# First batch of a rotary score kernel: eight-head groups with two row slots per step, and the third batch of k requested earlier

## The chip, the cores and the metric

The kernel runs on one core of one Trainium2 chip. The metric is device time in microseconds (µs): the median of several runs of the whole kernel. A profile of one execution is at hand; its span runs from the first to the last instruction, and its times count from the start of that span. All sizes are given in binary units (1 MB is 1024 KB), as the profile gives the sizes of transfers.

## What is computed

q and k have the shape 16 batches x 512 positions x 16 heads x 64 values, in float32. Both are rotated (rotary embedding), and then every position's q is multiplied with every position's k, head by head:

```
q1, q2 = q[..., :32], q[..., 32:]
q_rot = concatenate([q1*cos - q2*sin, q1*sin + q2*cos])      # k_rot likewise
scores = einsum('bshd,bthd->bsht', q_rot, k_rot)             # 16 x 512 x 16 x 512, float32
```

The output is 256 MB and the inputs are 64 MB, so the kernel moves much and computes little for each byte.

## The kernel before, in words

The 512 positions of a batch are split over 128 partitions of 4 positions each: partition p holds positions 4p to 4p+3. C is 4, the number of these row slots c. There are 64 steps `i`; from batch 1 on, step i is batch i // 4 and slot i % 4.

**One step from batch 1 on.** The rope of one slot of q (or k) is three VectorE (DVE) instructions (lines 149, 150, 154), which rotate the slot in place. TensorE (PE) transposes it in two groups `g` of four 128x128 blocks, each into a PSUM tile `bank` (line 170; two such buffers). A copy (line 185) takes each bank to `qT` or `kT` in SBUF, on ScalarE (ACT) or on DVE. `scores(i, p, st)` handles two heads: PE multiplies (line 201) into the PSUM tile `ps` (three buffers), and ACT copies ps to the staging tile `st` (line 208). After eight scores a 4 MB store goes out (line 188).

**The staging tiles.** `stage` has three buffers of 4 MB. The first two are `st_first`. The third first serves as `early`, which holds q and k of batch 0 until they are used; after that it too is a staging buffer. The third step waits until the stores of the first have landed.

**Batch 0** is treated differently, so that the first store can leave before all of batch 0 has arrived. A unit n (0 to 3) is a group of G = 4 heads in all four row slots, and it is loaded, roped and transposed as a unit: first unit 0 of k and of q (0.5 MB each), then units 1 to 3 (1.5 MB each), line 67. Step i of batch 0 computes all the scores of unit i: score p is row slot p // 2 and head pair p % 2 of the unit. After every second score a store of 1 MB leaves (line 211): 128 partitions, each with one run of 4 heads x 512 values x 4 bytes = 8 KB. So batch 0 has 16 stores.

**Order.** Nothing is reordered by a planner: instructions stand on each engine in the order in which the code is written (`manual_schedule`), and each engine works through its own in that order. In batch 0 the order is set by the loop over i and p: a list `dve` of rope halves, pieces of which are run at fixed p, and a list `nxt` of the two units to be transposed with ACT copies at p = 2 and p = 6. Beside unit i + 1 of k and q, step i also ropes slot i of batch 1's k, called ("k", C+i) in the code; it is transposed at p = 0 and 1 of the following step, with copies by DVE.

**Queues.** All loads and stores that matter here are issued by SyncE (SP), in the order of the code, and an issue that has to wait holds up those behind it. The order on SP in the first batch is: the four loads of batch 0, k of batch 1, q of batch 1 (all without a wait), two 1 MB stores, k of batch 2, four 1 MB stores, q of batch 2, ten 1 MB stores, k of batch 3, and then the 4 MB stores with two 2 MB loads in every batch. From batch 6 on a few loads go in parts through GpSimd's queue (`load_around`); the change does not touch them.

Of the kernel before, what the change touches and what calls it, by code (L numbers as in the profile page):

```python
# [10 lines left out]
def kernel(  # L11
# [8 lines left out]
    nc = tc.nc  # L20
# [7 lines left out]
    C = S // P  # L28
    HP = H // 2
    NST = B * C  # L30
    G = H // C
# [15 lines left out]
    o_v = out.rearrange("b (p c) h t -> b c p h t", c=C)  # L47
# [65 lines left out]
    def load(which, b):  # L113

        if b >= B:
            return
        t = in_pool.tile([P, C, H * D], fp32, tag=which + "_in", name=which + "_sb")
        batches[which, b] = t
        if (which, b) in RELIEVED:
            load_around(which, b, t)  # L120
        else:
            nc.sync.dma_start(t.rearrange("p c (h d) -> p c h d", h=H), dram[which][b])

    def rope(which, n):


        part = part_pool.tile([P, H * D], fp32, tag="part", name="part")
        if n < C:
            x = units[which, n]
            sv, k1, k2 = "p c (g j) -> p c g j", {"j": HD}, {"j": D}  # L130
            cs = cos_t.unsqueeze(2).to_broadcast((P, C, 2 * G, HD))
            ss = ss_v.unsqueeze(2).to_broadcast((P, C, G, D))
            pv = part.rearrange("p (c g j) -> p c g j", c=C, j=D)
            x5 = x.rearrange("p c (h x j) -> p c h x j", x=2, j=HD)
            p5 = part.rearrange("p (c h x j) -> p c h x j", c=C, x=2, j=HD)
            adds = [(x5[:, :, :, y], p5[:, :, :, 1 - y]) for y in range(2)]
        else:
            x = batches[which, n // C][:, n % C]
            sv, k1, k2 = "p (g j) -> p g j", {"j": HD}, {"j": D}
            cs = cos_t[:, n % C].unsqueeze(1).to_broadcast((P, 2 * H, HD))  # L140
            ss = ss_v[:, n % C].unsqueeze(1).to_broadcast((P, H, D))
            pv = part.rearrange(sv, **k2)
            x4 = x.rearrange("p (h x j) -> p h x j", x=2, j=HD)
            swapped = bass.AP(part.tensor, part.offset + HD, [part.ap[0], (D, H), (-HD, 2), (1, HD)])
            adds = [(x4, swapped)]
        xs, xc = x.rearrange(sv, **k2), x.rearrange(sv, **k1)

        def products():
            nc.vector.tensor_tensor(pv, xs, ss, op=mult)  # L149
            nc.vector.tensor_tensor(xc, xc, cs, op=mult)  # L150

        def sums():
            for y, z in adds:
                nc.vector.tensor_tensor(y, y, z, op=add)  # L154

        return [products, sums]

    kT = {}
    qT = {}

    def transposed(which, n, g, copy):


        bank = ps_t_pool.tile([P, 4, P], fp32, tag="ps_t", name="bank")
        for x in range(4):
            if n < C:
                src = units[which, n][:, x, P * g : P * (g + 1)]
            else:
                src = batches[which, n // C][:, n % C, P * (4 * g + x) : P * (4 * g + x + 1)]
            nc.tensor.transpose(bank[:, x, :], src, ident)  # L170
        src = bank
        if which == "q":
            if n not in qT:
                qT[n] = qt_pool.tile([P, HP, P], fp32, tag="qT", name="qT_t")
            dst = qT[n][:, 4 * g : 4 * g + 4, :]
        else:
            b = n // C
            if b not in kT:
                kT[b] = kt_pool.tile([P, HP, S], fp32, tag="kT", name="kT_t")
            if n < C:  # L180
                dst = kT[b][:, 2 * n + g].rearrange("p (t c) -> p t c", c=C)
                src = bank.rearrange("p c t -> p t c")
            else:
                dst = kT[b][:, 4 * g : 4 * g + 4, P * (n % C) : P * (n % C + 1)]
        copy(out=dst, in_=src)  # L185

    def store(i, st):
        nc.sync.dma_start(o_v[i // C, i % C], st)

    def scores(i, p, st):  # L190

        ps = ps_s_pool.tile([P, 2, S], fp32, tag="ps_s", name="ps")
        b = i // C
        if b == 0:
            c, hp = divmod(p, 2)
            lhs, rhs = qT[i][:, C * hp + c], kT[0][:, 2 * i + hp]
        else:
            lhs, rhs = qT[i][:, p], kT[b][:, p]
        for r in range(2):
            po, rh = ps[:, r, :], rhs[64 * r : 64 * r + 64, :]  # L200
            nc.tensor.matmul(  # L201
                out=po, lhsT=lhs[64 * r : 64 * r + 64, :], rhs=rh, start=True, stop=True
            )
        so, si = st[:, 2 * p : 2 * p + 2, :], ps
        if b > 0:
            so = so.rearrange("s r (t c) -> s r t c", c=C)
            si = si.rearrange("s r (c t) -> s r t c", c=C)
        nc.scalar.copy(out=so, in_=si)  # L208
        if b == 0 and p % 2 == 1:
            c = p // 2  # L210
            nc.sync.dma_start(o_v[0, c, :, G * i : G * (i + 1)], st[:, G * c : G * (c + 1)])
        elif b > 0 and p == HP - 1:
            store(i, st)

    def tr_act(which, n):
        for g in range(2):
            transposed(which, n, g, nc.scalar.copy)

    def run(ops):
        for op in ops:  # L220
            op()

    with tc.manual_schedule():
        for t, src in ((cos_t, cos), (sin_t, sin)):
            nc.scalar.dma_start(t, src.rearrange("(p c) j -> p c j", c=C))
        for head, heads in ((0, G), (G, H - G)):
            load_units("k", head, heads)
            load_units("q", head, heads)
        load("k", 1)
        load("q", 1)  # L230
        make_identity(nc, ident)
        nc.scalar.copy(out=ss_t[:, :, 0, :], in_=sin_t)
        nc.scalar.mul(ss_t[:, :, 1, :], sin_t, -1.0)
        for which in ("k", "q"):
            run(rope(which, 0))
            tr_act(which, 0)


        for i in range(C):
            st = st_first[i] if i < 2 else stage_pool.tile([P, H, S], fp32, tag="stage", name="st")  # L240
            if i < C - 1:
                dve = rope("k", i + 1) + rope("q", i + 1) + rope("k", C + i)
                nxt = [("k", i + 1), ("q", i + 1)]
            else:
                dve = rope("q", C) + rope("k", C + i) + rope("q", C + 1) + rope("k", 2 * C)
                nxt = [("q", C), ("k", C + i)]
            for p in range(HP):
                scores(i, p, st)
                if p in (0, 1) and i > 0:
                    run(dve[:1])  # L250
                    dve = dve[1:]
                    transposed("k", C + i - 1, p, nc.vector.tensor_copy)
                if p == 3 and i < 2:
                    load("kq"[i], 2)
                if p in (2, 6):
                    m = len(dve) - (4 if p == 2 else 2) - (2 if i == C - 1 else 0)
                    run(dve[:m])
                    dve = dve[m:]
                    tr_act(*nxt.pop(0))
            run(dve)  # L260
        load("k", 3)


        for i in range(C, NST):
            tr = {}
            if i + 1 < NST:
                tr[1], tr[3] = ("q", i + 1, 0), ("q", i + 1, 1)
            if i + C < NST:
                tr[5], tr[6] = ("k", i + C, 0), ("k", i + C, 1)
            dve = []  # L270
            if i + 2 < NST:
                dve += rope("q", i + 2)
            if i + 1 + C < NST:
                dve += rope("k", i + 1 + C)
            st = stage_pool.tile([P, H, S], fp32, tag="stage", name="st")
            for p in range(HP):
                scores(i, p, st)
                if p not in tr:
                    continue
                if tr[p][0] == "q":  # L280
                    run(dve[:1])
                    dve = dve[1:]
                    transposed(*tr[p], nc.vector.tensor_copy)
                else:
                    transposed(*tr[p], nc.scalar.copy)
            run(dve)
            if i % C == C - 2:
                load("q", i // C + 2)
            elif i % C == C - 1:
                load("k", i // C + 3)  # L290
# [30 lines left out]
```

## Time and profile before

| what | value |
|---|---|
| median of 3 runs | 793.13 µs (792.9 to 793.66) |
| span of the profiled execution | 790.4 µs |
| median less span, taken as what lies around the span | 2.7 µs |
| PE busy | 684.4 µs (87%) |
| DVE busy | 544.7 µs (69%) |
| ACT busy | 562.0 µs (71%) |
| moved by DMA | 336.18 MB (decimal), mean 425 GB/s |
| HBM read, written | 67.24 MB, 268.44 MB (decimal) |

The profile gives no second time for the profiled execution itself: what it shows is the span, and 790.4 + 2.7 µs is taken as its own time. The page cuts the span into 40 equal slices of 19.8 µs. Beside the engines' rows it has a row with the busy share of the 16 DMA engines in tenths (9 is 90% or more) and a row of what they moved. The timeline lists instructions in order of time; its rows for SP are the issues of transfers, and a row that merges several ("x10") has the time from the first issue to the end of the last. The trace also holds one record for each DMA packet, with its start, duration and size. One partition's run of a load or store is one packet, so the 1 MB stores have packets of 8 KB, the 2 MB loads of a whole batch 16 KB, and the 4 MB stores 32 KB. At the end of each transfer every one of the 16 engines has a small record of 4 bytes, the signal that its share is done.

### The profile page before, as it was taken

How to read it: one execution, taken by the hardware profiler on the slowest of the kernel's cores; microseconds unless marked ns; L12 is line 12 of the kernel's file. 1: busy time of each engine (PE TensorE's matmuls, PEld its weight loads, DVE VectorE, ACT ScalarE, POOL GpSimd, SP SyncE). 2: the span in 40 equal slices, each digit the busy share in tenths (PEclk: the TensorE clock that was granted, in tenths of full speed). 3: DMA queues.
4: the chain of work that ended last, by engine and by line, in shares of the span. 5: the costliest groups of instructions: out<-in, count | busy, mean ns of one | idle time of the engine just before them, and what ended most of it. 6: DMA issues, size and time to landing. Idle time of an engine off the chain costs nothing.

```text
span 790.4 us, 7750 instructions
## 1 busy us (share of the span) xinstructions
PE 684.4 (87%) x3072; PEld 296.4 (38%) x3072; DVE 544.7 (69%) x516; ACT 562.0 (71%) x647; POOL 11.9 (2%) x24
## 2 busy tenths in 40 slices
PE   4989998988988889798996989889899798799960
PEld 2444443433433334343342433334334343344420
DVE  6999988666766678576785767667678487587400
ACT  3888886865857768486785866777577586588770
POOL 0000000000001000000000001000000000000000
PEclk9999999998999999898998989999899899899995
DMA  9999999999999999999999999999999999999997
GB/s 357 417 425 439 429 430 435 425 435 436 429 429 428 413 432 419 433 423 438 433 427 436 426 432 429 422 432 424 430 432 427 436 429 432 430 432 434 432 429 340
DMA packets 18836, 336.18 MB, mean 425 GB/s; under 512 B 2312, under 2 KB 3592, under 8 KB 4616
## 3 DMA queue, kind: packets, MB, share of 16 engines
q1 hardware_dynamic: 16704, 325.46, 96.4%
q0 software_dynamic: 1808, 10.10, 3.1%
q8 instruction: 24, 0.39, 0.2%
q10 hardware_dynamic: 288, 0.13, 0.1%
q14 instruction: 12, 0.10, 0.0%
HBM read 67.24 MB, written 268.44 MB: 425 GB/s over the span
## 4 chain that ended last, share of the span: by engine, by line
DMA 49%; PE 40%; ACT 5%; DVE 3%; issue 1%; ACTq 0%; SPq 0%; DVEq 0%
DMA out_dram<-st 46%; PE ps L201 30%; PE bank L170 10%; ACT st L208 5%; DMA q_sb<-in_q_dram 2%; DVE part L149 1%; DMA early<-in_k_dram 1%; DVE q_sb L150 0%; DVE k_sb L154 0%; DVE k_sb L150 0%; DVE q_sb L154 0%; DVE early L150 0%; DVE kT_t L185 0%; ACTq L316 0%; DVE early L154 0%
## 5 line engine op out<-in xcount | busy, mean ns | idle before, releaser
L208 ACT COPY st<-ps 128x1024 f32<-128x1024 f32 x512 | 495.7, 1020 | 192.6 <-DMA out_dram<-st 109.8
L201 PE MATMUL ps<-kT_t,qT_t 64*128 64x512 f32 x2048 | 544.0, 649 | 67.0 <-ACT st L208 67.0
L201 PEld LDWEIGHTS ps<-kT_t,qT_t 64*128 64x128 f32 x2048 | 183.6, 196 | 256.2 <-issue 133.3
L185 DVE COPY qT_t<-bank 128x512 f32<-128x512 f32 x118 | 81.6, 691 | 193.9 <-PE bank L170 193.9
L170 PEld LDWEIGHTS bank<-ident,q_sb 128*128 128x128 f32 x480 | 54.2, 149 | 99.0 <-issue 96.4
L170 PEld LDWEIGHTS bank<-ident,k_sb 128*128 128x128 f32 x480 | 50.3, 140 | 96.4 <-DVE k_sb L150 39.5
L170 PE MATMUL bank<-ident,q_sb 128*128 128x128 f32 x480 | 85.1, 304 | 0.9 <-PE ps L201 0.9
L170 PE MATMUL bank<-ident,k_sb 128*128 128x128 f32 x480 | 78.5, 286 | 1.6 <-DVE qT_t L185 1.2
L185 ACT COPY kT_t<-bank 128x512 f32<-128x512 f32 x122 | 72.4, 598 | 6.4 <-PE bank L170 6.4
L154 DVE TENSOR_TENSOR k_sb<-k_sb,part 128x1024 f32<-128x1024 f32 x60 | 73.5, 1225 | 2.1
L150 DVE TENSOR_TENSOR q_sb<-q_sb,cos_t 128x1024 f32<-128x1024 f32 x60 | 73.5, 1225 | 2.1
L150 DVE TENSOR_TENSOR k_sb<-k_sb,cos_t 128x1024 f32<-128x1024 f32 x60 | 73.5, 1225 | 2.0
L149 DVE TENSOR_TENSOR part<-q_sb,ss_t 128x1024 f32<-128x1024 f32 x60 | 73.5, 1225 | 2.0
L149 DVE TENSOR_TENSOR part<-k_sb,ss_t 128x1024 f32<-128x1024 f32 x60 | 73.0, 1216 | 0.9 <-DMA k_sb<-in_k_dram 0.7
L154 DVE TENSOR_TENSOR q_sb<-q_sb,part 128x1024 f32<-128x1024 f32 x60 | 72.9, 1216 | 0.0
L170 PE MATMUL bank<-ident,early 128*128 128x128 f32 x64 | 10.5, 315 | 12.4 <-DVE early L154 10.5
L170 PEld LDWEIGHTS bank<-ident,early 128*128 128x128 f32 x64 | 8.3, 161 | 17.4 <-issue 13.4
L149 DVE TENSOR_TENSOR part<-early,ss_t 128x1024 f32<-128x1024 f32 x8 | 9.8, 1222 | 5.8 <-DMA early<-in_k_dram 5.7
L98 POOL DMA_DIRECT2D q_sb<-in_q_dram x3 | 2.3, 752 | 620.2 <-PE bank L170 446.2
L154 DVE TENSOR_TENSOR early<-early,part 128x512 f32<-128x512 f32 x16 | 10.3, 687 | 0.2
L150 DVE TENSOR_TENSOR early<-early,cos_t 128x1024 f32<-128x1024 f32 x8 | 9.8, 1225 | 0.3
L185 ACT COPY qT_t<-bank 128x512 f32<-128x512 f32 x10 | 5.7, 629 | 3.2 <-PE bank L170 3.2
(12 smaller groups left out, 15.9 us busy)
## 6 DMA issues: line engine op xcount, KB each, us to landing
out_dram<-st SPq DMA_DIRECT2D x60, 4096.0 KB, 24.7
k_sb<-in_k_dram SPq DMA_DIRECT2D x13, 2048.0 KB, 28.3
q_sb<-in_q_dram SPq DMA_DIRECT2D x12, 2048.0 KB, 26.5
out_dram<-st SPq DMA_DIRECT2D x16, 1024.0 KB, 13.8
q_sb<-in_q_dram POOLq DMA_DIRECT2D x3, 1920.0 KB, 27.8
k_sb<-in_k_dram POOLq DMA_DIRECT2D x2, 1920.0 KB, 43.3
early<-in_k_dram SPq DMA_DIRECT2D x1, 1536.0 KB
early<-in_q_dram SPq DMA_DIRECT2D x1, 1536.0 KB
```

Of the source, the lines that this page charges most:

```text
L98: nc.gpsimd.dma_start(dst, src)
L149: nc.vector.tensor_tensor(pv, xs, ss, op=mult)
L150: nc.vector.tensor_tensor(xc, xc, cs, op=mult)
L154: nc.vector.tensor_tensor(y, y, z, op=add)
L170: nc.tensor.transpose(bank[:, x, :], src, ident)
L185: copy(out=dst, in_=src)
L201: nc.tensor.matmul(out=po, lhsT=lhs[64 * r : 64 * r + 64, :], rhs=rh, start=True, stop=True)
L208: nc.scalar.copy(out=so, in_=si)
```

## The change

Batch 0 no longer goes unit by unit. `order[i]` lists for each step two units and two row slots: step 0 takes units 0 and 1 (heads 0 to 7) in slots 0 and 1, step 1 the same units in slots 2 and 3, step 2 units 2 and 3 in slots 0 and 1, step 3 the same in slots 2 and 3. Within a step the four scores of the lower unit come first (p = 0 to 3: two slots of two head pairs), then those of the upper one. A store leaves when the upper unit has finished a slot, after p = 5 and after p = 7: 2 MB, with runs of 8 heads, 16 KB. Batch 0 so has 8 stores in place of 16. The number of scores, ropes, transposes and copies stays the same.

The order by hand is now the table `plan`: after score (i, p) the listed operations follow. Two units' ropes come together, the transposes of batch 1's k come at p = 0 and 1 of the following step as before, and k of batch 2 is requested directly after q of batch 1, ahead of the first store. q of batch 2 follows the two stores of step 0.

```diff
+    E8 = 2 * G
+    order = [
+        [(2 * (i // 2) + u, 2 * (i % 2) + c, hp) for u in range(2) for c in range(2) for hp in range(2)]
+        for i in range(C)
+    ]
     def scores(i, p, st):
...
         if b == 0:
-            c, hp = divmod(p, 2)
-            lhs, rhs = qT[i][:, C * hp + c], kT[0][:, 2 * i + hp]
+            u, c, hp = order[i][p]
+            lhs, rhs = qT[u][:, C * hp + c], kT[0][:, 2 * u + hp]
+            at = E8 * (c % 2) + G * (u % 2) + 2 * hp
...
-        so, si = st[:, 2 * p : 2 * p + 2, :], ps
+        so, si = st[:, at : at + 2, :], ps
...
-        if b == 0 and p % 2 == 1:
-            c = p // 2
-            nc.sync.dma_start(o_v[0, c, :, G * i : G * (i + 1)], st[:, G * c : G * (c + 1)])
+        if b == 0 and u % 2 == 1 and hp == 1:
+            g = i // 2
+            nc.sync.dma_start(
+                o_v[0, c, :, E8 * g : E8 * (g + 1)], st[:, E8 * (c % 2) : E8 * (c % 2 + 1)]
+            )
...
         load("k", 1)
         load("q", 1)
+        load("k", 2)
...
+        plan = {
+            (0, 3): [("rope", "k", 1), ("act", "k", 1), ("rope", "q", 1), ("act", "q", 1)],
+            (0, 7): [("load", "q", 2), ("rope", "k", C)],
+            (1, 0): [("dve", "k", C, 0)],
+            (1, 1): [("dve", "k", C, 1), ("rope", "k", 2), ("rope", "q", 2)],
+            (1, 5): [("act", "k", 2)],
+            (1, 6): [("act", "q", 2)],
+            (1, 7): [("rope", "k", C + 1)],
+            (2, 0): [("dve", "k", C + 1, 0)],
+            (2, 1): [("dve", "k", C + 1, 1), ("rope", "k", 3), ("rope", "q", 3)],
+            (2, 3): [("act", "k", 3), ("act", "q", 3)],
+            (2, 7): [("rope", "k", C + 2)],
+            (3, 0): [("dve", "k", C + 2, 0)],
+            (3, 1): [("dve", "k", C + 2, 1), ("rope", "q", C), ("rope", "k", C + 3)],
+            (3, 4): [("act", "q", C)],
+            (3, 6): [("act", "k", C + 3)],
+            (3, 7): [("rope", "q", C + 1), ("rope", "k", 2 * C)],
+        }
         for i in range(C):
...
-            if i < C - 1:
-                dve = rope("k", i + 1) + rope("q", i + 1) + rope("k", C + i)
-                nxt = [("k", i + 1), ("q", i + 1)]
-            else:
-                dve = rope("q", C) + rope("k", C + i) + rope("q", C + 1) + rope("k", 2 * C)
-                nxt = [("q", C), ("k", C + i)]
             for p in range(HP):
                 scores(i, p, st)
-                if p in (0, 1) and i > 0:
-                    run(dve[:1])
-                    dve = dve[1:]
-                    transposed("k", C + i - 1, p, nc.vector.tensor_copy)
-                if p == 3 and i < 2:
-                    load("kq"[i], 2)
-                if p in (2, 6):
-                    m = len(dve) - (4 if p == 2 else 2) - (2 if i == C - 1 else 0)
-                    run(dve[:m])
-                    dve = dve[m:]
-                    tr_act(*nxt.pop(0))
-            run(dve)
+                for what, which, n, *g in plan.get((i, p), ()):
+                    if what == "rope":
+                        run(rope(which, n))
+                    elif what == "load":
+                        load(which, n)
+                    elif what == "act":
+                        tr_act(which, n)
+                    else:
+                        transposed(which, n, g[0], nc.vector.tensor_copy)
```

In `plan`, "rope" runs the three or four DVE instructions of a unit or slot, "act" its transposes with copies by ACT, "dve" one group of transposes with a copy by DVE, and "load" a request on SP.

More of the change, by code (lines that the diff above doesn't have):

```diff
@@ L194, in scores @@
         if b == 0:
-            c, hp = divmod(p, 2)
-            lhs, rhs = qT[i][:, C * hp + c], kT[0][:, 2 * i + hp]
+            u, c, hp = order[i][p]
+            lhs, rhs = qT[u][:, C * hp + c], kT[0][:, 2 * u + hp]
+            at = E8 * (c % 2) + G * (u % 2) + 2 * hp
         else:
-            lhs, rhs = qT[i][:, p], kT[b][:, p]
+            lhs, rhs, at = qT[i][:, p], kT[b][:, p], 2 * p
         for r in range(2):
```

## The prediction

> **What bounds the kernel now.** I read the page's rows by slices first. The sixteen DMA engines are full from the second slice to the last but one.
>
> ```profile
> DMA  9999999999999999999999999999999999999997
> GB/s 357 417 425 439 429 430 435 425 435 436 429 429 428 413 432 419 433 423 438 433 427 436 426 432 429 422 432 424 430 432 427 436 429 432 430 432 434 432 429 340
> q1 hardware_dynamic: 16704, 325.46, 96.4%
> ```
>
> So the time is start-up, plus bytes at about 430 GB/s, plus a tail. Nothing is won on PE, ACT or DVE; but whatever lets the DMA queue run empty is added to the end in full, for no later stretch has room to make it good. Next the engines' busy time in the stretch of the change, four windows of 20 µs (columns: PE, PEld, DVE, ACT, POOL with counts, then clock, DMA share, GB/s):
>
> ```profile
> 0.00:20.00 20.00, 8.51 (x35) 5.48 (x36) 13.95 (x15) 6.66 (x10) 1.39 (x7) 1.00 0.91 354
> 20.00:40.00 20.00, 20.00 (x105) 9.48 (x103) 19.40 (x21) 16.65 (x22) 0.00 (x0) 1.00 1.00 419
> 40.00:60.00 20.00, 17.91 (x93) 8.59 (x92) 19.62 (x22) 16.85 (x21) 0.00 (x0) 1.00 1.01 425
> 60.00:80.00 20.00, 18.75 (x92) 8.24 (x92) 19.66 (x19) 16.28 (x20) 0.00 (x0) 1.00 1.04 441
> ```
>
> DVE is busy 97 to 98% there: the ropes set when batch 0's stores can leave. A pause of DVE delays everything after it. The SP timeline shows when transfers are requested (first column; a merged row gives its first issue):
>
> ```profile
> 19.52 3.28 SPq L211 DMA_DIRECT2D out_dram<-st  x2
> 22.85 0.66 SPq L122 DMA_DIRECT2D k_sb<-in_k_dram  x1
> 24.29 9.39 SPq L211 DMA_DIRECT2D out_dram<-st  x4
> 33.73 0.84 SPq L122 DMA_DIRECT2D q_sb<-in_q_dram  x1
> 35.18 27.44 SPq L211 DMA_DIRECT2D out_dram<-st  x10
> 62.72 0.57 SPq L122 DMA_DIRECT2D k_sb<-in_k_dram  x1
> 73.69 20.37 SPq L188 DMA_DIRECT2D out_dram<-st  x3
> ```
>
> Stores wait for ACT's copies, not for SP. And DVE's timeline gives the starts of the ropes of k1, k2, q2, k3, q3 (units), the rows to be moved:
>
> ```profile
> 13.37 1.23 DVE L149 TENSOR_TENSOR part<-early,ss_t 128x1024 f32<-128x1024 f32 x1
> ...
> 24.84 1.22 DVE L149 TENSOR_TENSOR part<-early,ss_t 128x1024 f32<-128x1024 f32 x1
> ...
> 29.92 1.22 DVE L149 TENSOR_TENSOR part<-early,ss_t 128x1024 f32<-128x1024 f32 x1
> ...
> 37.54 1.22 DVE L149 TENSOR_TENSOR part<-early,ss_t 128x1024 f32<-128x1024 f32 x1
> ...
> 42.34 1.22 DVE L149 TENSOR_TENSOR part<-early,ss_t 128x1024 f32<-128x1024 f32 x1
> ```
>
> **DMA's side of the change.** The packet records give the commonest times: 27 ns for 0.5 KB, 46 for 1 KB, 121 for 3 KB, 309 for 8 KB, 611 for 16 KB, 1213 for 32 KB. Sixteen engines share 128 partitions, so a 2 MB load takes 128 x 611 / 16 = 4.89 µs, a 1 MB store 2.47, a 2 MB store 4.89, a 4 MB store 9.70; cos and sin together 0.43, a 0.5 MB load of batch 0 1.47, a 1.5 MB load 3.87.
>
> The runs: 2048 packets x 309 ns / 16 = 39.55 µs become 1024 x 611 / 16 = 39.10. **Gain 0.45 µs**, and 8 completion records of 9 ns per engine fall away, 0.07. I take 0.5.
>
> The Trainium skill ("DMA: Bandwidth & Descriptors", Anatomy of one DMA) fits 2.0 µs plus bytes / 436 GB/s to one transfer issued by GpSimd; by that, eight transfers fewer would save 16 µs. This trace disagrees: stores that stand in the queue follow one another at 2.45 µs per 1 MB (428 GB/s), so the fixed part is hidden and the sum goes by the packets.
>
> When does the queue run dry? With an effective start at 2.6 µs (first packet at 2.18, then a ramp), cos, sin, batch 0 and k and q of batch 1 end at 2.6 + 0.43 + 2 x 1.47 + 2 x 3.87 + 2 x 4.89 = 23.5; the completion records of that last load lie between 23.47 and 24.48. Eight 1 MB stores and k and q of batch 2 more give 53.05; the records there lie from 52.8 (eleven engines by 53.3) to 55.1 (the slowest). The account holds. **After the change:** k of batch 2 now ends at 28.4, the two stores of step 0 at 38.2, q of batch 2 at 43.1, the two stores of step 1 at **52.9**. The next bytes must be requested before that, less the delay from request to first packet: 0.74 to 2.18 = 1.4 µs at the start of the kernel. Below, it can't be less than a store's issue, 0.33; above, with the ramp, I allow 2. I take 1.4, the only row; the ends would make the first gap below 4.9 or 6.6.
>
> **Compute's side.** Durations: a unit's rope 3.85 µs (starts 9.52 and 13.37), a slot's 3.78, a DVE copy between them 0.50, ACT's copy of ps 0.94, of a bank 0.56, one score on PE 0.86 plus 0.2 after a change from transposes, a bank of four transposes 0.59. I walked all instructions in order with these through both codes. For the code before, the walk puts k of batch 3 at 62.83 (trace 62.72), the first 4 MB store at 73.87 (73.69), the fourth at 103.99 (103.74), and no dry queue.
>
> *Step 0.* The ropes up to slot 0 of batch 1's k keep their times: q1 ends at 21.04, that slot at 24.85. Scores 0 to 3 leave ACT by 21.3; the copies of k1's and q1's banks end at 23.7, scores 4 and 5 at 26.3. First store: **26.4** (was 19.52), data at 27.8. The earlier request of k of batch 2 covers just this: dry at 28.4, 0.6 µs in hand; it costs nothing else, being queued behind all loads that batches 0 and 1 need, and its issue of 0.66 µs falls where SP would wait for ACT anyway. Without it the queue would stand from 23.5. The second store goes out at 28.3.
>
> *The new wait.* DVE's next instruction is now the copy of batch 1's transposed k. PE makes that bank only after scores 4 to 7 of step 0 and one of step 1: ready at 28.6. DVE stands from 24.85, **3.75 µs**, and 1.15 more for the second bank (one more score and transpose). Before, k2's rope stood at 24.84 and the copies lay inside. What is queued behind is everything: k2's rope begins at 30.7 (24.84), q2's at 34.6 (29.92) and ends at 38.4.
>
> *Steps 1 and 2.* Step 1's first store comes at 35.0, its second, after k2's and q2's transposes, at 41.7; both are in time. The same wait returns at the start of step 2 (0.9 + 1.15 µs): k3 begins at 45.3 (37.54), q3 at 49.1 (42.34), ending at 53.0. Step 2's first store needs unit 3: transposes, two bank copies, scores 4 and 5, 4.6 µs more. It is requested at **57.55**, its data come at 58.95, and the queue ran dry at 52.9: **6.0 µs lost**. In the profile before, 1 MB stores of step 2 were requested from about 42 on, since unit 2 alone sufficed. The copy of step 2 that waited for step 0's stores (2.61 µs until 40.59) has no wait now: they land at about 40 (38.2 and the 1.8 that landing took there), and that copy comes at 43.6.
>
> *Step 3 and after.* DVE waits again for its copies (3.0 + 1.15 µs). From step 2's first store to step 3's first, compute takes 11.4 µs (57.55 to 68.97), the two stores between 9.8: 1.6 lost. Then two stores and k of batch 3 (14.7 µs) against 15.8 until the first 4 MB store at 84.76 (was 73.69): 1.1 lost. Steps now run at 10.04 µs against 9.71 for a 4 MB store: 0.33 lost twice, until the q load fills the queue again. Before, there were about 4 µs in hand at 73.69 (stores and k of batch 3 end at 77.8); the change delays compute there by 11.
>
> Sum: 6.0 + 1.6 + 1.1 + 0.3 + 0.3 = 9.3 lost, 0.5 gained. One correction: two engines run 1.5 and 2.1 µs behind the rest at 53 µs and so stand less in the first gap. If one of these ends the kernel, the loss is up to 2 smaller; the last store's records spread from 783.6 to 789.0, and I can't tell which engine is last. I take 0.6 off: **+8.2 µs**. The profiled execution has 790.4 + 2.7 around it; that is the median, 793.1, so 801.3.
>
> **The rivals.**
> 1. *Only the large gap counts* (0.15). The four small gaps fall away, by a compute that is a little quicker than walked or by lagging engines that never stand: 6.0 - 2 - 0.5 = +3.5, 796.6. For it: the small ones total 3.3 µs, and errors of 0.1 to 0.2 µs per step are seen in the check. Against: they come from differences of durations (10.04 against 9.71), which the check confirms.
> 2. *Not slower: the queue never runs dry* (0.06). One mechanism: DVE does not wait at the starts of steps 1 and 2, so that step 2's first store is requested before 51.5 (52.9 - 1.4). It decides from 6 µs earlier than walked; the two waits are 6.95 together, so both must vanish. Then only the packets count: -0.5, 792.6; at best, if all packets of the stretch from 20 to 60 µs ran at 430 GB/s in place of 422, -0.8 more. Against: PE's order puts those banks behind the scores, and in the profile before PE and ACT had no time to spare there.
> 3. *The first store is late too* (0.07). Only 0.6 µs of cover stands at 28.4; should the new run of transposes and scores take 4 µs longer, a gap of about 3 opens there and the rest is pushed back: +11.5, 804.6.
>
> Forecast 0.72: 801.3. The range takes in rivals 1 and 3: 796.5 to 804.6. A difference under 0.2% (1.6 µs) can't be told from no change in measurements of this kernel; rival 2 splits into same 0.04 and faster 0.02, the rest, 0.94, is slower.
>
> **What the changed profile would show.** Right: the DMA row drops to 7 or 8 in the third slice (39.5 to 59.3) and the GB/s there falls to about 300 (6 of 19.8 µs at 430), the two after it to some 400; step 2's first store is issued at 57 to 58; DVE has idle time ahead of line 185 (kT) released by PE, some 11 µs in all; the first 4 MB store is issued near 85; the slices from the sixth on are unchanged; span near 798.6. Wrong: a third slice at 9 and stores of step 2 issued before 52; a dip near 28 speaks for rival 3; a single dip, with full slices from the fourth on, for rival 1. What would overthrow it altogether is a changed packet time in the later slices, which nothing here moves.

## The result, and the profile after

| | before | after |
|---|---|---|
| median of 5 runs each, side by side | 793.13 µs (792.78 to 793.84) | 806.32 µs (805.21 to 806.58) |
| ratio, 95% interval | | 1.0161 (1.0149 to 1.0173) |
| span of the profiled execution | 790.4 µs | 804.7 µs |
| its own time | not shown | 806.47 µs |

The changed kernel is 13.2 µs slower, 1.6%. The forecast was 801.3 (796.5 to 804.6): the direction is right, the size is not, and the range misses the time by 1.7 µs. The spans differ by 14.3 µs and the medians by 13.2. For the kernel after, 1.8 µs lie around the span (806.47 less 804.7); with 1.8 in place of the 2.7 that the prediction took, the profiled execution of before ran about 0.9 µs quicker than its median, and the one of after 0.15 µs slower, which together is that difference. The steps below are set against the 14.3.

First the page of the kernel after, its rows by slices and the queue that holds the loads and stores:

```profile
DMA  9969999999999999999999999999999999999997
GB/s 351 430 269 390 415 395 415 429 430 438 423 434 425 390 428 426 437 431 424 437 433 428 430 433 427 402 435 421 436 432 429 437 425 432 432 432 432 429 434 333
q1 hardware_dynamic: 15552, 325.46, 95.1%
```

A slice is 20.1 µs now. The third one, from 40.2 to 60.4, has a 6 where before had a 9, and 269 GB/s. It is the only digit that moved, but the figures below it show more: 390 in the fourth slice, 395 in the sixth, 390 in the fourteenth. Next the requests on SP in the timeline of the kernel after (start, duration, and how many):

```profile
26.41 0.35 SPq L218 DMA_DIRECT2D out_dram<-st  x1
28.25 0.34 SPq L218 DMA_DIRECT2D out_dram<-st  x1
34.97 0.33 SPq L218 DMA_DIRECT2D out_dram<-st  x1
41.73 0.33 SPq L218 DMA_DIRECT2D out_dram<-st  x1
59.75 0.33 SPq L218 DMA_DIRECT2D out_dram<-st  x1
61.62 9.96 SPq L218 DMA_DIRECT2D out_dram<-st  x2
75.52 0.91 SPq L122 DMA_DIRECT2D k_sb<-in_k_dram  x1
87.00 0.33 SPq L188 DMA_DIRECT2D out_dram<-st  x1
```

The four stores of steps 0 and 1 were predicted at 26.4, 28.3, 35.0 and 41.7, and they came there. Step 2's first was predicted at 57.55 and came at 59.75. The first 4 MB store is at 87.00, 13.3 µs later than before; the prediction had 84.76. The DVE timeline of the kernel after shows why (the bracket is the idle time ahead of an instruction, and what ended it):

```profile
28.47 0.69 DVE L185 COPY kT_t<-bank 128x512 f32<-128x512 f32 x1 [3.62 <-PE bank L170]
30.12 0.69 DVE L185 COPY kT_t<-bank 128x512 f32<-128x512 f32 x1 [0.95 <-PE bank L170]
30.73 1.22 DVE L149 TENSOR_TENSOR part<-early,ss_t 128x1024 f32<-128x1024 f32 x1
...
42.97 0.69 DVE L185 COPY kT_t<-bank 128x512 f32<-128x512 f32 x1 [0.81 <-PE bank L170]
44.61 0.69 DVE L185 COPY kT_t<-bank 128x512 f32<-128x512 f32 x1 [0.95 <-PE bank L170]
45.22 1.22 DVE L149 TENSOR_TENSOR part<-early,ss_t 128x1024 f32<-128x1024 f32 x1
...
61.97 0.69 DVE L185 COPY kT_t<-bank 128x512 f32<-128x512 f32 x1 [5.32 <-PE bank L170]
```

DVE stands for the transposed k of batch 1 at the start of each step, and the ropes of k2 and k3 start at 30.73 and 45.22, as predicted (30.7, 45.3). Up to 53 µs the walk was right to 0.2 µs. What it missed stands in the windows of 2 µs of the kernel after (columns as in the prediction: engines, clock, DMA share, GB/s):

```profile
50.00:52.00 2.00, 0.23 (x3) 0.00 (x0) 1.93 (x3) 0.91 (x2) 0.00 (x0) 0.98 0.96 410
52.00:54.00 2.00, 0.99 (x5) 1.02 (x6) 1.97 (x3) 0.00 (x0) 0.00 (x0) 0.50 0.44 188
54.00:56.00 2.00, 2.00 (x9) 1.16 (x9) 1.93 (x3) 1.17 (x2) 0.00 (x0) 0.50 0.06 25
56.00:58.00 2.00, 2.00 (x8) 0.91 (x6) 0.65 (x1) 0.99 (x1) 0.00 (x0) 0.50 0.00 0
58.00:60.00 2.00, 2.00 (x10) 0.82 (x8) 0.00 (x0) 1.30 (x3) 0.00 (x0) 0.82 0.00 0
60.00:62.00 2.00, 2.00 (x14) 0.84 (x12) 0.03 (x1) 2.00 (x3) 0.00 (x0) 1.00 0.93 393
```

PE waits for the rope of q3 and is nearly idle until 53.0; its granted clock is then 0.50 until 58 and 0.82 between 58 and 60. The transposes and scores that step 2's first store needs run in just that time, and the DMA queue stands: nothing is requested, and its engines idle. What the clock does to them is seen on PE's timeline, in the eight transposes of k3 and the eight of q3:

```profile
49.17 1.06 PE L170 MATMUL bank<-ident,early 128*128 128x128 f32 x8 [2.68 <-DVE early L154]
53.01 1.94 PE L170 MATMUL bank<-ident,early 128*128 128x128 f32 x8 [2.78 <-DVE early L154]
```

**Where the 14.3 µs of span are**, from the packet records, as means over the 16 engines:

| term | µs |
|---|---|
| the queue stands, 52.9 to 60.6 | 7.3 |
| it stands again at 70.3 to 72.1 | 1.6 |
| and at 87.3, 97.5 and 107.6 | 0.8 |
| smaller stands | 0.2 |
| packets that took longer than the commonest of their size: 10.3 against 5.9 before | +4.4 |
| the sum of the commonest durations (fewer, longer packets) | -0.5 |
| idle engines after 770 µs | +0.3 |
| packet records that overlap on an engine: 3.8 against 4.0 before | +0.2 |
| sum | 14.3 |

In the profile of e10 below, the same kernel once more, the stands sum to 9.9 as here, the longer packets to +3.8 and the idle tail to +1.2: these two terms differ by 0.6 to 0.9 µs between two executions of one kernel.

### The profile page after: what moved, and what is told of

It reads as the page before. It is cut to its first block, busy times and chain, and to the rows that moved or that the text cites. A ratio compares the mean times of both kernels' runs of the same rounds, so it can differ in the third digit from the quotient of the medians.

```text
span 804.7 us, 7732 instructions
## 1 busy us (share of the span) xinstructions
PE 686.3 (85%) x3072; PEld 298.4 (37%) x3072; DVE 545.2 (68%) x516; ACT 563.3 (70%) x647; POOL 12.0 (1%) x24
## 4 chain that ended last, share of the span: by engine, by line
DMA 46%; PE 40%; ACT 5%; DVE 5%; issue 1%; ACTq 0%; DVEq 0%
DMA out_dram<-st 46%; PE ps L208 30%; PE bank L170 10%; ACT st L215 5%; DVE part L149 2%; DVE early L150 1%; DVE early L154 1%; DMA early<-in_k_dram 1%; DVE k_sb L154 0%; DVE k_sb L150 0%; DVE q_sb L150 0%; DVE q_sb L154 0%; DVE kT_t L185 0%; ACT kT_t L185 0%; ACTq L335 0%
## 5 line engine op out<-in xcount | busy, mean ns | idle before, releaser
L170 PEld LDWEIGHTS bank<-ident,k_sb 128*128 128x128 f32 x480 | 50.3, 140 | 96.5 <-issue 40.2
L154 DVE TENSOR_TENSOR q_sb<-q_sb,part 128x1024 f32<-128x1024 f32 x60 | 72.9, 1216 | 0.1
L170 PE MATMUL bank<-ident,early 128*128 128x128 f32 x64 | 11.3, 333 | 20.3 <-DVE early L154 17.7
L185 DVE COPY kT_t<-bank 128x512 f32<-128x512 f32 x6 | 4.2, 692 | 12.6 <-PE bank L170 12.6
L154 DVE TENSOR_TENSOR early<-early,part 128x512 f32<-128x512 f32 x16 | 10.3, 688 | 0.3
```

## The experiments

The theory was the prediction's: DVE's copies of batch 1's k, put ahead of the next ropes, make it wait for banks that PE makes only behind a run of scores; compute falls behind by more than the queue has in hand, the queue runs dry, and that is never made good. The rivals: the early request of k of batch 2 does it; the pairing does it, since a 2 MB store needs two units; the 16 KB runs do it (rival C). After the result two more questions came up: what PE's halved clock costs, and where the 4.4 µs of longer packets come from. Medians are set against the kernel before on the same chip: 793.08, 793.38 and 793.76 in the three groups (e1 to e4, e5 to e8, e9 to e11).

**e1: the early request alone.** The kernel before, with k of batch 2 requested right after q of batch 1.

```diff
         load("q", 1)
+        load("k", 2)
...
-                if p == 3 and i < 2:
-                    load("kq"[i], 2)
+                if p == 3 and i == 1:
+                    load("q", 2)
```

> The kernel before, with one part of the change alone: k of batch 2 is requested directly after q of batch 1. Theory A (the loss comes from DVE standing ahead of the kT copies, which makes compute late): compute keeps its times, the queue never runs dry, 793.1 within 0.7. Rival (a load of 2 MB ahead of the first stores pushes the early stores back and makes the third step wait for staging): step 2 waits up to 4.9 longer for the stores of step 0, up to 798.

Measured: 793.23 (792.25 to 794.15), ratio 1.0002 (0.9993 to 1.001); the queue never stands. Moving the request into a full queue costs nothing. It isn't the cause.

**e2: the changed kernel without the early request.** k of batch 2 follows step 0's two stores.

```diff
-        load("k", 2)
...
-            (0, 7): [("load", "q", 2), ("rope", "k", C)],
+            (0, 7): [("load", "k", 2), ("load", "q", 2), ("rope", "k", C)],
```

> The changed kernel, with k of batch 2 requested after the two stores of step 0 instead of ahead of the first. Theory A: the queue stands for about 4 near 24 to 28, but the stand before step 2's first store shrinks from 7.3 to about 3.3, since the same bytes are moved by the same late requests; total 806.3 within 1.5. Rival (each stand adds up; the early request is worth its cover): 806.3 + 4 = 810.

Measured: 806.54 (806.48 to 806.62), 1.017 (1.0157 to 1.0183), the changed kernel's time. The page of e2:

```profile
DMA  9798999999999999999999999999999999999997
GB/s 356 324 370 377 406 408 415 427 438 431 423 437 425 393 430 427 436 434 423 440 430 430 432 429 429 416 430 422 433 430 432 432 425 435 430 434 429 430 437 325
```

The hole moves: 4.1 µs at 23.4 to 27.7 (the second slice), then only 2.1 at 58.6, 1.7 at 70.8 and three of 0.3. They sum to 8.8 µs, and the span is 804.7 in both kernels. A queue that stood early has more left to send later, so the later hole is smaller. The request is harmless, and under a compute that is late anyway it is worth nothing.

**e3: the ropes back in front of the copies.** The changed kernel, with DVE's list in an order that keeps it busy: the next unit's rope before the first copy, the first instruction of the other unit's rope between the two ("products"; "sums" are the rest).

```diff
-            (0, 7): [("load", "q", 2), ("rope", "k", C)],
-            (1, 0): [("dve", "k", C, 0)],
-            (1, 1): [("dve", "k", C, 1), ("rope", "k", 2), ("rope", "q", 2)],
+            (0, 7): [("load", "q", 2), ("rope", "k", C), ("rope", "k", 2)],
+            (1, 0): [("dve", "k", C, 0), ("products", "q", 2)],
+            (1, 1): [("dve", "k", C, 1), ("sums", "q", 2)],
...
```

Steps 2 and 3 are changed in the same way. Pairs, 2 MB stores and the early request stay.

> The changed kernel with DVE's order turned back: k2's rope (and k3's, and q of batch 1's first) goes ahead of the two kT copies, and the second copy stands between the two halves of the next rope. Pairs of units, 2 MB stores, 16 KB runs and the early request all stay. Theory A: DVE does not stand, step 2's first store is issued near 50.6 instead of 59.75, the first 4 MB store near 73.6 instead of 87.0, the queue never runs dry, 792.6 within 1. Rival B (stores that need two units are the cause): the queue still runs dry before step 2, 797 to 806. Rival C (packets of 16 KB and engines in step are slower): 795 to 798 without any stand.

Measured: 793.46 (792.0 to 795.84, 12 runs), 1.001 (1.0 to 1.0021). The page of e3:

```profile
DMA  9999999999999999999999999999999999999997
GB/s 355 430 426 434 428 433 431 424 438 434 428 430 430 419 434 415 436 423 433 438 422 437 433 427 434 412 434 418 435 426 428 440 428 427 429 438 432 429 437 310
```

And its requests on SP, step 2's first store, k of batch 3 and the first 4 MB stores:

```profile
50.35 0.33 SPq L218 DMA_DIRECT2D out_dram<-st  x1
63.34 1.13 SPq L122 DMA_DIRECT2D k_sb<-in_k_dram  x1
73.33 20.36 SPq L188 DMA_DIRECT2D out_dram<-st  x3
```

Step 2's first store leaves before the queue is dry (52.9), the 4 MB store is 13.7 µs earlier than in the changed kernel, and the queue never stands. The whole loss is gone with the order on one engine alone; it decides for the theory. (Four of the 12 runs lie at 795.1 to 795.8, the others at 792.0 to 793.9; the profile is of one of the latter, and what sets the four apart is open.) The 0.5 µs of longer runs are not to be seen in it: 793.46 against 793.08.

**e4: no pairing of stores.** The changed kernel, but 1 MB leaves whenever a unit's slot is ready, so batch 0 has 16 stores of 8 KB runs again.

```diff
-        if b == 0 and u % 2 == 1 and hp == 1:
+        if b == 0 and hp == 1:
...
-                o_v[0, c, :, E8 * g : E8 * (g + 1)], st[:, E8 * (c % 2) : E8 * (c % 2 + 1)]
+                o_v[0, c, :, G * u : G * (u + 1)], st[:, E8 * (c % 2) + G * (u % 2) : E8 * (c % 2) + G * (u % 2 + 1)]
```

> The changed kernel's order of work, but each unit's slot leaves as soon as it is copied, in 16 stores of 1 MB with 8 KB runs. Theory A: stores leave earlier, compute stays late; the stand before step 2's upper unit shrinks to about 3, but stands appear before the stores of step 3 and the first 4 MB store (near 83 to 88), and the total stays at 806 within 1.5. Rival B (pairing is the cause): most of the loss goes, 794 to 800.

Measured: 805.81 (805.48 to 806.44), 1.0162 (1.0149 to 1.0175); span 804.7. The stands are now 2.4 at 57.5, 1.5 at 70, 1.4 at 74, 3.6 at 84 to 87 and two of 0.3, 9.4 in all. Smaller stores start earlier and fill part of the first hole, and the time shows up as another hole ahead of the first 4 MB store. Neither the pairing nor the 16 KB runs are the cause.

**e5: 2 MB in two stores of 8 KB runs.** Issued together, after the upper unit.

```diff
-            nc.sync.dma_start(
-                o_v[0, c, :, E8 * g : E8 * (g + 1)], st[:, E8 * (c % 2) : E8 * (c % 2 + 1)]
-            )
+            for x in range(2):
+                nc.sync.dma_start(
+                    o_v[0, c, :, E8 * g + G * x : E8 * g + G * (x + 1)],
+                    st[:, E8 * (c % 2) + G * x : E8 * (c % 2) + G * (x + 1)],
+                )
```

> The changed kernel with each 2 MB store of batch 0 cut into two of 1 MB (8 KB runs) that are requested one after the other at the same moment. Theory A (late compute): nothing moves but 0.45 of packet time, 806.3 within 1. Rival C (16 KB runs or large stores are themselves slower): 804 or less.

Measured: 807.82 (805.5 to 808.62), 1.0178 (1.0161 to 1.0194). It isn't a clean test: the lower half waits only for its own copies, so the first store left at 20.61 instead of 26.41, and in the profiled execution the first rope began 0.4 µs later (6.12 against 5.72). It gives no sign for rival C, which needed 804 or less, but the effect of the packet size alone isn't isolated by it.

**e6 and e11: PE kept warm.** The changed kernel with 20 and 22 transposes of the identity into the bank, ahead of k3's and q3's own transposes (which then overwrite them). e11 is the same kernel once more, beside e10, the changed kernel once more, on one chip.

```diff
+    WARM = {("k", 3, 0): 20, ("q", 3, 0): 22}
...
+        for x in range(WARM.get((which, n, g), 0)):
+            nc.tensor.transpose(bank[:, x % 4, :], ident, ident)
```

> The changed kernel with 20 and 22 additional transposes of the identity (overwritten by the real ones) ahead of the transposes of k3 and q3, so that PE does not stand while DVE ropes them. If the halved granted clock of PE at 52 to 58 is what put step 2's first store 2.2 later than the 57.55 of the prediction, that store now goes out near 57.7, the stand before it shrinks from 7.3 to about 5.3, and all later requests come 2 earlier: 804.3 within 0.8. Rival (the clock does not matter; the prediction's walk was off elsewhere): 806.3.

> The changed kernel once more, beside the next one on the same chip: 806.3 within 1, stands of 9 to 10.5 in all, packet records longer than before's by 3.5 to 5.5 for each engine.

> The changed kernel with the additional transposes that keep PE busy, once more: if the halved clock is worth the 2.6 by which step 2's first store came earlier, 2 to 3 below the changed kernel of this call. Rival (it only moves stands about): the same as the changed kernel within 1.

Measured: e6 804.32 (802.98 to 806.23), 1.014 (1.0123 to 1.0157); e10 806.53 (806.02 to 807.25), 1.0166 (1.0151 to 1.0181); e11 803.74 (803.33 to 804.29), 1.013 (1.0115 to 1.0145). The windows of e11:

```profile
50.00:52.00 2.00, 2.00 (x19) 2.00 (x20) 1.97 (x3) 0.35 (x1) 0.00 (x0) 1.00 1.00 426
52.00:54.00 2.00, 1.76 (x15) 1.39 (x15) 1.93 (x3) 0.88 (x2) 0.00 (x0) 1.00 0.27 115
54.00:56.00 2.00, 2.00 (x10) 0.84 (x10) 1.97 (x2) 1.26 (x3) 0.00 (x0) 1.00 0.04 8
56.00:58.00 2.00, 2.00 (x12) 0.77 (x8) 0.15 (x1) 2.00 (x3) 0.00 (x0) 1.00 0.30 131
```

The clock stays at 1.00 and step 2's first store is requested at 56.89, 2.8 µs before e10's 59.72 and near the 57.55 of the prediction. The stands fall from 9.9 to 7.2 µs and the time by 2.8 (806.53 to 803.74, and the ranges don't overlap). Not all of that is the clock: in the profiled executions 0.47 µs of the earlier store was there before the first added transpose (the first copy of k starts at 27.98 in e11, at 28.45 in e10). From the start of q3's transposes to the request it is 4.46 µs in e11 and 6.74 in e10, so the halved clock costs 2.3 µs on this chain; 2.8 is what the medians show.

**e7: one stand, elsewhere.** The kernel before, with 44 small copies on ACT, whose result nobody reads, ahead of step 6, so that a single 4 MB store is late.

```diff
+            if i == C + 2:
+                for _ in range(44):
+                    nc.scalar.copy(out=scratch[:, 64:96], in_=cos_t[:, 0, :])
```

> The kernel before with 44 small additional ACT copies ahead of step 6's, some 9 in all, so that the queue runs dry once, before the store of step 6 (near 97 to 104), and with nothing else changed. It asks whether a stand costs more than its length. If a stand costs its length alone: median = 793.1 + the stand read from the trace (some 6). If the 16 DMA engines, restarted together, then work in step and stretch one another's packets where loads and stores meet: 2 to 4 more than the stand, with the packet records of 100 to 290 longer than in the kernel before.

Measured: 804.71 (804.1 to 805.31), 1.0141 (1.0124 to 1.0157), span 803.5. The windows of e7, 4 µs each, around the stand and behind it:

```profile
92.00:96.00 4.00, 0.00 (x0) 0.00 (x0) 0.00 (x0) 3.62 (x15) 0.00 (x0) 0.50 0.97 418
96.00:100.00 4.00, 3.98 (x10) 1.72 (x12) 0.82 (x2) 2.81 (x3) 0.00 (x0) 0.50 0.21 90
100.00:104.00 4.00, 4.00 (x20) 1.67 (x16) 3.90 (x4) 2.88 (x4) 0.00 (x0) 0.91 0.00 0
104.00:108.00 4.00, 4.00 (x21) 1.89 (x22) 2.53 (x3) 3.85 (x5) 0.00 (x0) 1.00 0.31 131
116.00:120.00 4.00, 4.00 (x24) 1.68 (x20) 2.66 (x3) 3.48 (x5) 0.00 (x0) 1.00 0.68 266
```

The queue stands for 9.7 µs (mean of the engines, 96.6 to 107.1) instead of the 6 that were aimed at: PE idled here too and restarted at 0.50. The last row is no second stand: a packet is counted in the window in which it starts, the 16 engines began their 32 KB packets just before 116 µs (115.57 to 115.72), and the packet records show next to no idle time from 112 to 124 (0.03 µs). The span grew by 13.2: 9.7 of stand, 2.5 of longer packets, 0.9 at the tail. Between medians it is 11.3, the firmer number, for the profiled execution was the longest of e7's four. So with nothing else changed a stand of 9.7 costs 1.7 to 3.5 µs more than its length, and packets lengthen in a kernel that has neither pairs nor 16 KB stores.

**e8: the kernel before with the changed DVE order.** The two lines that run one rope instruction before each copy are taken out.

```diff
                 if p in (0, 1) and i > 0:
-                    run(dve[:1])
-                    dve = dve[1:]
                     transposed("k", C + i - 1, p, nc.vector.tensor_copy)
```

> The kernel before with one part of the change alone: DVE makes the two kT copies of a step ahead of the next rope, instead of between its halves; DVE's order is then that of the changed kernel, while units, 1 MB stores and requests stay as before. Theory A: DVE stands for PE, the first 4 MB store goes out near 81.7 instead of 73.7, the queue stands for some 5.7 in all (near 66, 79, 92 and 102), and with 2 to 4 of stretched packets the total is 799 to 803. Rival B (pairing is the cause, DVE's order alone is harmless): 793 to 795.

Measured: 806.16 (804.39 to 807.99), 1.0162 (1.0142 to 1.0182), above the 799 to 803 that was expected. The waits of the changed kernel and of e8 up to 110 µs have these rows (total, times, longest):

```profile
DVE kT_t L185 <- PE bank L170: 12.6, 6, 5.3
DVE kT_t L185 <- PE bank L170: 11.0, 6, 3.3
```

and its windows show the hole:

```profile
40.00:60.00 20.00, 16.46 (x74) 8.20 (x72) 13.98 (x15) 13.00 (x17) 0.00 (x0) 0.83 0.99 416
60.00:80.00 20.00, 16.58 (x72) 8.15 (x72) 17.67 (x16) 12.47 (x16) 0.00 (x0) 0.83 0.66 273
```

DVE waits 11.0 µs in six places (12.6 in the changed kernel, 0.2 in one place in the kernel before), the 4 MB store comes at 87.50 (87.00), and the queue stands 9.7 µs, mostly at 66.4 to 72.9. The expectation had left PE's clock at full, which is 0.83 in both windows, and had no term for longer packets, which take 3.6 µs more here than in the kernel before (9.5 against 5.9). With units of four heads, 1 MB stores and the old request of k, the order on DVE alone makes the whole loss.

**e9: what the early request is worth when compute is in time.** e3, with k of batch 2 after step 0's stores.

```diff
-        load("k", 2)
...
-            (0, 7): [("load", "q", 2), ("rope", "k", C), ("rope", "k", 2)],
+            (0, 7): [("load", "k", 2), ("load", "q", 2), ("rope", "k", C), ("rope", "k", 2)],
```

> The kernel of the run with the ropes first (no DVE stand, no dry queue, 793.5), with k of batch 2 requested after the two stores of step 0. The loads end near 23.5 and the first store's data come near 27.3, so the queue stands once for about 4. If a stand counts in full where compute is not late afterwards: 797.2, and with 1.5 to 3 of stretched packets after it 798 to 800.5. Rival (the early request is worth nothing, as it was in the changed kernel): 793.5.

Measured: 798.29 (797.51 to 799.57), 1.0067 (1.005 to 1.0083). One stand of 3.4 µs at 23.5 to 27.2, and nothing after it. Against e3 that is 4.8 µs between medians (4.2 when each is set against the kernel before on its own chip), 4.5 between spans (795.7 and 791.2): again more than the stand. The early request does pay for the later first store, but only where no later request decides.

**The longer packets.** The packet records show when each engine starts its 32 KB packets, which take 1213 ns. In the kernel before their starts are spread over 0.92 to 0.97 µs of these 1.21 among the 16 engines. After a stand all engines start together: in e10 the starts lie within 0.14 to 0.34 µs at 90 to 110 µs. Where a load then borders on stores, packets lengthen. Windows of the changed kernel over the first such load of 2 MB:

```profile
112.00:116.00 4.00, 4.00 (x22) 1.83 (x20) 3.90 (x4) 3.78 (x5) 0.00 (x0) 1.00 0.91 393
116.00:120.00 4.00, 4.00 (x20) 1.49 (x16) 3.32 (x4) 3.47 (x4) 0.00 (x0) 1.00 1.01 340
120.00:124.00 4.00, 4.00 (x22) 1.83 (x20) 3.25 (x5) 3.42 (x5) 0.00 (x0) 1.00 0.97 315
```

and of the kernel before over the same load:

```profile
104.00:108.00 4.00, 4.00 (x22) 1.90 (x22) 2.67 (x4) 3.47 (x4) 0.00 (x0) 1.00 0.96 414
108.00:112.00 4.00, 4.00 (x22) 1.76 (x20) 3.90 (x5) 3.34 (x5) 0.00 (x0) 1.00 1.06 451
```

The engines are as busy in both (share about 1), but they move 315 to 340 GB/s in place of 414 to 451: the load's 16 KB packets take 754 ns on average, where 611 is the commonest, and the 32 KB packets beside it 1345 for 1213 (before: 614 and 1219). The excess of all packets over the commonest durations is 5.7 to 6.0 µs per engine in the three profiles without a stand (before, e1, e3), and 7.2 to 11.1 in the ten with one or more.

That a stand brings longer packets is shown by e7 (8.4 against 5.9), by e9 against e3 (7.2 against 6.0) and by the gap between the two sets, though one kernel's two profiles lie 0.7 apart. That the engines' working in step is the way it does so is only argued from the starts and the places. It is not clear-cut there either: the 16 engines begin the load above within 0.69 µs of each other, and within 0.91 in the kernel before. A stand after which the engines restart out of step wasn't tried, and the mechanism stays open.

## Why the prediction was right in sign and wrong in size

The mechanism held; two terms of the sum did not. Step 2's chain was walked with PE at full clock, and the packets were taken to keep their common durations behind a dry queue. Step by step:

- **What bounds the kernel, and that a dry queue is never made good**: right. Wherever the holes lie (e2, e4), the total is about the same, 8.8 to 9.9 µs of stands, and the span is 804.7 in all three. It is set by the last request at which the queue is empty: the 4 MB store is 13.3 µs late, and the account before had 4.1 in hand there (77.8 less 73.69). That leaves 9.2, with the small stands of the following steps to add.
- **The new wait on DVE**: right, in place and cause, and in size but for one. Five of the six waits came within 0.2 µs of the walk; the first of step 3 was 5.32 for 3.0, behind a PE at 0.50, and so the sum is 12.6 for some 11. e3 and e8 show that it alone makes and unmakes the loss.
- **The early k and the first store's cover of 0.6 µs**: right (no stand at 28; e9 shows 3.4 µs of stand without it). Rival 3 falls.
- **Step 2's chain to its first store** ("4.6 µs more"): the failed term of compute's side. Its durations were those of a PE at full clock, but the walk itself left PE idle ahead of 53 µs. At 0.50 the transposes and scores took 6.74 µs, 2.1 longer: 59.75 in place of 57.55. With the clock kept at 1.00 they took 4.46 (e11). The first stand is 7.3 in place of 6.0; data followed the request by 0.84 µs, not the 1.4 taken, which gave some of it back. That 1.4 was not "the only row": in the same profile cos is requested at 0.74 and its first packet starts at 1.74, 1.0 µs later.
- **The small gaps**: 1.6 as predicted, then 0.8 for the predicted 1.1 + 0.3 + 0.3. All stands sum to 9.9 against 9.3. Rival 1 falls, and with it the low end of the range. That the two sums lie so close is luck: with the clock at 1.00 the stands are 7.2 (e11), 2.1 below the sum, and the halved clock, which the walk left out, hid that.
- **"A changed packet time in the later slices, which nothing here moves"**: this is the step that failed most; the sum had no term for it. Packets took 4.4 µs more per engine (3.8 in e10), and the range had no room for it, because the packets had been priced at the commonest durations of a queue that never stood.
- **The correction of 0.6 for lagging engines**: not seen; idle time at the tail grew by 0.3.
- **The gain of 0.5 from longer runs**: the sum of commonest durations does fall by 0.5, but no time shows it (e3).

So the prediction's 8.2 became 14.3: 0.6 more of stands, 4.4 of packets, 0.6 of a correction that isn't there, 0.3 of tail and 0.2 of overlaps. Either missing piece alone, the packets' 4.4 or the clock's 2.3 to 2.8, is more than the 1.7 µs by which the time lies above the range. No version beat the kernel before; e1 and e3 equal it.

## What to carry to other kernels

Before moving an instruction that waits for another engine to the head of an in-order list, look at what is queued behind it: here two copies of 0.7 µs in each of three steps, put ahead of the ropes, cost 13 µs. Where DMA is the bound, ask for the lateness of the last request that finds the queue empty; filling an earlier hole, or cutting transfers smaller, only moves the time as long as such a later request decides (e2 and e4, against e9). And price a hole at more than its length: the engines that idle meanwhile may restart slower, and the transfers behind it too.

## What the runs showed that was not expected

- PE idled for 2.7 and 2.8 µs (46.5 to 49.2 and 50.2 to 53.0), and its granted clock fell to 0.50. In the profile of the changed kernel that lasted from 51.9 to 58.7 µs; in e10, the same kernel, from 48.6 to 58.8, so there it fell before the second began. Keeping PE busy with useless transposes took 2.8 µs off the time (e11 against e10).
- After a stand the 16 DMA engines run in step, and packets at the border of loads and stores lengthen (754 ns for 611 in one load); by 130 to 150 µs the starts are spread again (over 0.6 to 0.9 µs).
- A store into an empty queue had its first data 0.84 to 0.86 µs after its request (the changed kernel, e7, e9), against 1.0 and 1.4 for the first loads of the kernel.
